# Order of up-projection pieces and down-projection products in the feed-forward part of a hybrid attention layer

## The chip, the cores and the metric

The kernel runs on one core of one Trainium2 chip. The metric is device time in microseconds (us), taken as the median of several runs.

## The reference

One layer of a hybrid encoder, on 256 tokens of width 2048, all in float32. First a mixer with two groups of eight heads (forgetting attention and stick-breaking attention), then the feed-forward part, which the change is about:

```python
def conv_ffn(h, w_up_l, conv_w_l, conv_b_l, w_down_l):
    u = h @ w_up_l                       # (256, 2048) @ (2048, 2 * 5632)
    u = causal depthwise conv of width 3 over tokens, + conv_b_l
    gate, val = jnp.split(u, 2, axis=-1)
    return (jax.nn.silu(gate) * val) @ w_down_l   # (256, 5632) @ (5632, 2048)
...
h = rms_norm(x, ffn_norm[layer])
x = x + conv_ffn(h, w_up[layer], conv_w[layer], conv_b[layer], w_down[layer])
```

## The kernel before

**Numbers in two halves.** Every float32 matrix is used as a high part (a cast to fp32r) and a low part (what the cast left over). A product then takes high x high, high x low and low x high. Weights are split on the chip as they arrive: `split` (L201, L202) casts the raw tile to `w_hi` on ACT, and subtracts it from the raw tile on DVE to get `w_lo`. Activations are kept as pairs, in `hT` (the layer's input, features by tokens) and `g` (the gated features).

**Up-projection.** The 5632 hidden features are taken in six parts of 8 blocks of 128 (the last has 4). For each two blocks there is a gate and a val half, and each of these is one *up-pair*: two *up-pieces*, the first over features 0 to 1023 of the input, the second over 1024 to 2047. A piece (`from_features`) issues 16 high products (L250, 512 columns: both parts of `hT` against `w_hi`) and 16 low products (L257, 256 columns: the high part of `hT` against `w_lo`), all into the tile `pu`. After the second piece, `convolved` and what follows it work on the finished tile: a copy on ACT, an addition (L835) and a multiplication by the token factors on DVE (L837), the three taps on ACT, their sums on DVE (L856), the SiLU or the product with the gate, and the split into high and low parts.

**Down-projection.** Each part's down-projection is done while the next part's up-projection runs. For each half of the output columns, `down_in_seven` forms a 2 x 2 block product with seven products in place of eight. I call the seven A1 to A7 for the first half and B1 to B7 for the second; in the code they are the seven calls of `product`, in order. Each is 12 matmuls (L223) into a PSUM bank. The banks: products 1, 4, 5 and 7 accumulate into `bank_a`, 2 and 6 into `bank_b`, and 3 is `bank_c`. After each product the running sum in its bank is added into, or subtracted from, a block of x by DVE (`added`, L933); the next product on that bank adds to the sum that was read there. Products 2, 4 and 7 use a weight sum, `w_sum`: DVE makes it first (`first_sum`, L986), and two further weights are added into it by accumulating DMAs from the POOL queue (`plus`, L956), which also add into the raw tile of the second weight, used by product 5. Products 2, 4, 5 and 6 take sums of gated features as the other operand (tiles `s`, L898 and L903).

**Order.** All this is a list of steps, each an up-piece or a down-product. The string `ORDER` says how they follow each other in a part (`u` an up-piece, `s` a down-product, a digit the plain down-projection of the last part), `LAST_ORDER` the same for the last part. Letters for which nothing is left are passed over: in the first part there is no `s`. A loop then issues, for step n in the middle, on queues that keep exactly this order:

```python
at(LOAD, 0)      # DMA of the raw weights of step n + 6
follow()         # one move of all that follows finished steps
at(SPLIT, 2)     # split of step n + 2
follow()
at(SUM, 1)       # weight sum of step n + 4
at(0, 3)         # matmuls of step n
```

What follows a step (`convolved`, `added`, and so on) are generators that move on by one `yield` at each `follow()`, the oldest first. There are four raw tiles (`w_raw`), three `w_hi` and three `w_lo`, so the split of step n + 3 goes into the tiles that step n has read. The attention stage before uses `from_features` too, through `feature_major`, in eight pairs of pieces with two `w_hi` and two `w_lo`.

Of the kernel before, what the change touches and what calls it, by code (L numbers as in the profile page):

```python
# [14 lines left out]
P = 128  # L15
D = 2048
S = 256
NT = S // P
KT = D // P
# [18 lines left out]
FFN_PARTS = [(f, min(f + 8, NFT)) for f in range(0, NFT, 8)]  # L38


ORDER = "uuusususususususususususususus"
LAST_ORDER = "uususususususussss0s1ss3s2"


@with_exitstack
def hybrid_layer(
# [19 lines left out]
    nc = tc.nc  # L66
# [65 lines left out]
    hT = big.tile([P, KT, 2, S], F32R, name="hT")  # L132
# [98 lines left out]
    def token_major(lhs, w, k0, nk, c0, cols):  # L231

        acc = psa.tile([P, NT, 512], F32, name="acc", tag="acc")
        for k in range(0, nk, 4):
            parts = weights(rows_of(w, k0 + k, 4, c0, cols), 4, cols)
            in_three(
                [acc[:, t, :cols] for t in range(NT)], parts, 4,
                lambda i, part, t: of_half(lhs(k + i), part, t), k == 0, k + 4 == nk,
            )
            step()  # L240
        return acc

    def from_features(acc, parts, kh, n=8):

        hi, lo = parts
        for i0 in range(0, 8, n):
            for i in range(i0, i0 + n):
                k = 8 * kh + i
                for j in range(2):
                    nc.tensor.matmul(  # L250
                        acc[:, j, :], hi[:, i, j * P : (j + 1) * P],
                        hT[:, k].rearrange("p a b -> p (a b)"), start=k == 0, stop=False,
                    )
            for i in range(i0, i0 + n):
                k = 8 * kh + i
                for j in range(2):
                    nc.tensor.matmul(  # L257
                        acc[:, j, S:], lo[:, i, j * P : (j + 1) * P], hT[:, k, 0, :],
                        start=False, stop=k == KT - 1,
                    )  # L260

    def feature_major(w, c0, pool, tag):

        acc = pool.tile([P, 2, 512], F32, name="pu", tag=tag)
        for kh in range(2):
            from_features(acc, weights(rows_of(w, 8 * kh, 8, c0, 2 * P), 8, 2 * P), kh)
            step()
        return acc
# [9 lines left out]
    with ExitStack() as actx:  # L278
# [9 lines left out]
        def project(c0, cols):  # L288
            return token_major(lambda k: hT[:, k], wi, 0, KT, c0, cols)
# [199 lines left out]
        low = big.tile([P, 2, 16 * P], F32R, name="low", tag="x2")  # L489
# [41 lines left out]
        for j in range(3):  # L531
            acc = project(2 * WF + 344 * j, 344)
            n = 344 if j < 2 else 336
# [206 lines left out]
        for half in range(2):  # L740
            qT = sb_queries(half)
            kT = sb_keys(half)
            acc = project(B0 + 2 * WF + 512 * half, 512)
# [18 lines left out]
        for group in range(2):  # L762
# [3 lines left out]
            for c in range(4):  # L766
                acc = token_major(lambda k: oT[group * NH + k], wo, group * NH, NH, 512 * c, 512)
# [6 lines left out]
                if c == 0:  # L774
                    pg = psb.tile([P, NT], F32, name="pg", tag="t")
                    for t in range(NT):
                        nc.tensor.matmul(
                            pg[:, t : t + 1], ssq[group][:, t * P : (t + 1) * P], ones[:, 0:1],
                            start=t == 0, stop=t == NT - 1,
# [125 lines left out]
    def up_pieces(part, f0, follows):  # L905

        c0 = f0 * P + (DFF if follows is val_follows else 0)
        cell = []

        def piece(kh):  # L910
            mem = {}

            def loads():
                mem["raw"] = load(rows_of(wu, 8 * kh, 8, c0, 2 * P))

            def prepare():
                mem["parts"] = split(mem["raw"], 8, 2 * P)

            def matmuls():
                if kh == 0:  # L920
                    cell.append(psa.tile([P, 2, 512], F32, name="pu", tag="acc"))
                from_features(cell[0], mem["parts"], kh, 8 if c0 else 4)

            new_step(loads, None, prepare, matmuls, (lambda: follows(part, cell[0], f0)) if kh else None)

        piece(0)
        yield
        piece(1)
        yield
# [76 lines left out]
    def down_plain(part, c):  # L1006

        n = (part.f_hi - part.f_lo) // 4

        ends = LAST_ORDER[-1] == str(c // 512)  # L1010
        sizes = [(0, 0, 512), (1, 0, 256), (1, 256, 256)] if ends else [(t, 0, 512) for t in range(NT)]
# [45 lines left out]
    for f_lo, f_hi in FFN_PARTS:  # L1057
# [9 lines left out]
        if f_hi == NFT:  # L1067
            steps_of |= {str(i): [down_plain(part, 512 * i)] for i in range(4)}
        for g in ORDER if f_hi < NFT else LAST_ORDER:
            if steps_of[g]:  # L1070
# [83 lines left out]
```

## Time and profile before

| | before |
|---|---|
| runs | 1107.03, 1107.19, 1107.64 us (median 1107.19) |
| profiled execution, first to last instruction | 1104.9 us |
| PE (matmul) busy | 1099.6 us, 5880 matmuls |
| DVE busy | 870.4 us |
| ACT busy | 706.3 us |

The profiled execution has its span only, from its first to its last instruction; a run's time lies 2.1 to 2.7 us above it (1107.03 to 1107.64 against 1104.9). Times of a row are a start in us after the span's beginning, a length in us, the engine, the line, and what is written from what. PE is the matrix engine, PEld its weight loads, DVE the vector engine, ACT the scalar engine, POOL and SP the engines that issue DMAs. `[2.62 <-PE pu L250]` says that the engine stood idle for 2.62 us before, until PE finished with `pu` at L250. Matmuls are pipelined: a row's length contains the end of the last one, so the pace is read from start to start. In groups, the columns are the count, then busy us and the mean in ns of one, then idle time before and what ended it.

### The profile page before, as it was taken

The page shows a single profiled execution, that of the slowest core. Times are in us where ns is not written, and L with a number is a line of the kernel's source. Part 1 is how long each engine was busy: PE and PEld are TensorE (multiplying, and loading weights), DVE is VectorE, ACT ScalarE, POOL GpSimd, SP SyncE. Part 2 cuts the span into 40 slices and gives each one's busy share as a digit, 9 for nine tenths or more (in the row PEclk, how much of TensorE's full clock was granted, in tenths as well). Part 3 has the DMA queues.
Part 4 walks back from the last instruction along what each step waited for, and adds up shares of the span by engine and source line. Part 5 has one row for each costly group of instructions (what it writes and reads, how often), then busy time and mean ns, then how long its engine had stood idle before and what let it go on. Part 6 is the DMA issues. An engine that isn't in the chain of part 4 may idle for free. (4 is left out here: it accounts for less than half of the span.)

```text
span 1104.9 us, 14836 instructions
## 1 busy us (share of the span) xinstructions
PE 1099.6 (100%) x5880; PEld 953.9 (86%) x5880; DVE 870.4 (79%) x941; ACT 706.3 (64%) x879; POOL 44.0 (4%) x44
## 2 busy tenths in 40 slices
PE   9999999999999999999999999999999999999998
PEld 7998888888888888888888888888888888888887
DVE  6755767667676677679889888889798889889896
ACT  6543555457674567667767776667676677677753
POOL 0000000000000000000000010100000010100010
PEclk9999999999999999999999999999999999999999
DMA  8776555555644396557989597986979689987985
GB/s 285 195 232 229 187 164 180 173 170 169 242 156 158 114 304 200 190 189 195 301 210 323 191 229 264 260 269 178 315 210 306 213 218 281 245 264 196 324 212 168
DMA packets 179407, 246.09 MB, mean 223 GB/s; under 512 B 4432, under 2 KB 118890, under 8 KB 179082
## 3 DMA queue, kind: packets, MB, share of 16 engines
q1 hardware_dynamic: 162458, 209.87, 58.3%
q0 software_dynamic: 16560, 34.75, 16.7%
q8 instruction: 46, 0.75, 0.3%
q10 hardware_dynamic: 320, 0.53, 0.1%
q14 instruction: 23, 0.19, 0.0%
HBM read 243.02 MB, written 2.11 MB: 222 GB/s over the span
## 5 line engine op out<-in xcount | busy, mean ns | idle before, releaser
L202 DVE TENSOR_TENSOR w_lo<-w_raw,w_hi 128x2048 fp32r<-128x2048 f32 (+1 forms) x196 | 439.7, 2246 | 155.0 <-ACT w_hi L201 153.2
L201 ACT CAST w_hi<-w_raw 128x2048 fp32r<-128x2048 f32 (+1 forms) x196 | 367.1, 1875 | 247.4 <-PE pu L250 68.9
L250 PE MATMUL pu<-hT,w_hi 128*128 128x512 f32 x1664 | 396.7, 390 | 0.0
L250 PEld LDWEIGHTS pu<-hT,w_hi 128*128 128x128 f32 x1664 | 309.4, 188 | 62.6
L257 PEld LDWEIGHTS pu<-hT,w_lo 128*128 128x128 f32 x1664 | 213.7, 191 | 8.3
L257 PE MATMUL pu<-hT,w_lo 128*128 128x256 f32 x1664 | 216.4, 283 | 0.0
L223 PE MATMUL acc<-w_hi,hT 128*128 128x512 f32 (+1 forms) x576 | 124.9, 369 | 0.0
L223 PEld LDWEIGHTS acc<-w_hi,hT 128*128 128x128 f32 x576 | 101.2, 188 | 14.2
L201 ACT CAST w_hi<-w_sum 128x2048 fp32r<-128x2048 f32 x30 | 57.2, 1908 | 42.0 <-PE pu L250 35.8
L202 DVE TENSOR_TENSOR w_lo<-w_sum,w_hi 128x2048 fp32r<-128x2048 f32 x30 | 68.7, 2290 | 19.0 <-ACT w_hi L201 19.0
L851 ACT ACTIVATE tap<-up,ccol 128x256 f32<-128x256 f32 x176 | 74.6, 495 | 0.0
L223 PE MATMUL acc<-w_lo,hT 128*128 128x512 f32 (+1 forms) x288 | 64.6, 366 | 0.0
L223 PEld LDWEIGHTS acc<-w_lo,hT 128*128 128x128 f32 x288 | 51.6, 188 | 7.5
L956 POOL DMA_DIRECT2D w_sum<-in_w_down_dram x20 | 25.7, 1284 | 742.8 <-DVE w_lo L202 732.1
L223 PE MATMUL acc<-w_hi,oT 128*128 128x512 f32 x192 | 46.5, 394 | 0.0
L223 PEld LDWEIGHTS acc<-w_hi,oT 128*128 128x128 f32 x192 | 35.4, 188 | 7.2
L223 PE MATMUL bank_a<-w_hi,s 128*128 128x512 f32 x160 | 40.1, 392 | 0.2 <-DVE x L933 0.2
L223 PE MATMUL bank_a<-w_hi,g 128*128 128x512 f32 x160 | 40.0, 392 | 0.0
L223 PE MATMUL bank_b<-w_hi,s 128*128 128x512 f32 x160 | 40.0, 392 | 0.0
L223 PEld LDWEIGHTS bank_a<-w_hi,s 128*128 128x128 f32 x160 | 28.8, 189 | 5.8 <-issue 0.6
L223 PEld LDWEIGHTS bank_a<-w_hi,g 128*128 128x128 f32 x160 | 28.9, 189 | 5.3
L223 PEld LDWEIGHTS bank_b<-w_hi,s 128*128 128x128 f32 x160 | 28.9, 189 | 5.2
(215 smaller groups left out, 1077.5 us busy)
## 6 DMA issues: line engine op xcount, KB each, us to landing
w_raw<-in_w_up_dram SPq DMA_DIRECT2D x88, 1024.0 KB, 7.9
w_raw<-in_w_down_dram SPq DMA_DIRECT2D x44, 1024.0 KB, 6.6
w_raw<-in_w_in_dram SPq DMA_DIRECT2D x36, 1024.0 KB, 5.3
w_sum<-in_w_down_dram POOLq DMA_DIRECT2D x20, 1024.0 KB, 10.3
w_raw<-in_w_out_dram SPq DMA_DIRECT2D x16, 1024.0 KB, 5.1
w_raw<-in_w_down_dram POOLq DMA_DIRECT2D x10, 1024.0 KB, 14.7
w_raw<-in_w_in_dram SPq DMA_DIRECT2D x12, 688.0 KB, 4.3
w_raw<-in_w_in_dram SPq DMA_DIRECT2D x6, 512.0 KB, 7.1
```

The costliest lines, as they stand in the source:

```text
L201: act.copy(hi[:, :n], raw[:, :n])
L202: dve.tensor_tensor(lo[:, :n], raw[:, :n], f32(hi[:, :n]), op=ALU.subtract)
L223: nc.tensor.matmul(o, lhs(i, l, t), r[:, i, :], start=starts and j == 0, stop=stops and j == 3 * n - 1, skip_group_check=more,)
L250: nc.tensor.matmul(acc[:, j, :], hi[:, i, j * P : (j + 1) * P], hT[:, k].rearrange("p a b -> p (a b)"), start=k == 0, stop=False,)
L257: nc.tensor.matmul(acc[:, j, S:], lo[:, i, j * P : (j + 1) * P], hT[:, k, 0, :], start=False, stop=k == KT - 1,)
L851: act.activation(taps[w][:, j, :], u[:, j, w : w + S], AF.Copy, scale=ccol[:, w, f : f + 1])
L956: nc.gpsimd.dma_start(mem[into][:, : nk * 512].rearrange("p (a b) -> p a b", a=nk), src, accum_op=ALU.add)
```

## The change

Two things change. In `from_features` the second piece of a pair (`kh` is 1) issues its low products before its high ones, so that a pair goes high, low, low, high. And the orders are rewritten: the two pieces of a pair follow each other directly, and two down-products stand between pairs, where one stood between pieces.

```diff
-ORDER = "uuusususususususususususususus"
-LAST_ORDER = "uususususususussss0s1ss3s2"
+ORDER = "uuuu" + "ssuu" * 6 + "ss"
+LAST_ORDER = "uussuussuussuussss0s1ss3s2"
...
     def from_features(acc, parts, kh, n=8):
 
         hi, lo = parts
+
+        def high(k, i, j):
+            nc.tensor.matmul(
+                acc[:, j, :], hi[:, i, j * P : (j + 1) * P],
+                hT[:, k].rearrange("p a b -> p (a b)"), start=k == 0, stop=k == KT - 1,
+            )
+
+        def low(k, i, j):
+            nc.tensor.matmul(
+                acc[:, j, S:], lo[:, i, j * P : (j + 1) * P], hT[:, k, 0, :], start=False, stop=False,
+            )
+
         for i0 in range(0, 8, n):
-            for i in range(i0, i0 + n):
-                k = 8 * kh + i
-                for j in range(2):
-                    nc.tensor.matmul(
-                        acc[:, j, :], hi[:, i, j * P : (j + 1) * P],
-                        hT[:, k].rearrange("p a b -> p (a b)"), start=k == 0, stop=False,
-                    )
-            for i in range(i0, i0 + n):
-                k = 8 * kh + i
-                for j in range(2):
-                    nc.tensor.matmul(
-                        acc[:, j, S:], lo[:, i, j * P : (j + 1) * P], hT[:, k, 0, :],
-                        start=False, stop=k == KT - 1,
-                    )
+            for product in (low, high) if kh else (high, low):
+                for i in range(i0, i0 + n):
+                    for j in range(2):
+                        product(8 * kh + i, i, j)
```

## The prediction

> **What bounds the kernel now.** I read the page first (busy times, then the slices), then busy time by stage, then the order of time of each engine in one cycle.
>
> ```profile
> PE 1099.6 (100%) x5880; PEld 953.9 (86%) x5880; DVE 870.4 (79%) x941; ACT 706.3 (64%) x879; POOL 44.0 (4%) x44
> PEclk9999999999999999999999999999999999999999
> ```
> ```profile
> 504.00:621.00 117.00, 117.00 (x625) 101.30 (x624) 103.78 (x94) 84.67 (x95) 7.77 (x6) 1.00 0.90 253
> 631.00:749.00 118.00, 118.00 (x629) 102.17 (x629) 102.59 (x90) 83.94 (x92) 7.74 (x6) 1.00 0.91 254
> ```
> The columns of the second fence are the stage, its length, and the busy time of PE, PEld, DVE, ACT and POOL. In the stages where up-pieces and down-products alternate, PE has no idle time at all and DVE is busy 103.8 of 117.0 us, 89%. So PE sets the time, a microsecond in which PE waits is a microsecond lost, and DVE is the engine that can make it wait.
>
> One cycle on PE, in order of time (start, length, operation):
> ```profile
> 573.55 3.79 PE L250 MATMUL pu<-hT,w_hi 128*128 128x512 f32 x16
> 577.18 2.08 PE L257 MATMUL pu<-hT,w_lo 128*128 128x256 f32 x16
> 579.09 2.00 PE L223 MATMUL bank_c<-w_hi,g 128*128 128x512 f32 x8
> 580.93 1.07 PE L223 MATMUL bank_c<-w_lo,g 128*128 128x512 f32 x4
> 581.84 3.79 PE L250 MATMUL pu<-hT,w_hi 128*128 128x512 f32 x16
> ```
> From start to start: 16 high products 3.63 us, 16 low ones 1.91, so an up-piece is 5.54; a down-product is 2.75. That is 227 ns a high product and 119 ns a low one, through the changes of kind too.
>
> **The change part by part.**
>
> *Low products first: no gain.* The same matmuls and weight loads are issued. A change from high to low and back costs nothing visible (3.63 + 1.91 is 16 x 227 + 16 x 119), so setting two low runs side by side removes nothing. Taken at 0.
>
> *What it moves: the release of w_hi.* A second piece now reads its high half last, so that buffer comes free at the end of the piece, 1.91 us later. How the next split hangs on that release is seen here, on ACT and on DVE:
> ```profile
> 577.38 1.91 ACT L201 CAST w_hi<-w_sum 128x2048 fp32r<-128x2048 f32 x1 [2.62 <-PE pu L250]
> ```
> ```profile
> 579.35 2.29 DVE L202 TENSOR_TENSOR w_lo<-w_sum,w_hi 128x2048 fp32r<-128x2048 f32 x1 [2.27 <-ACT w_hi L201]
> 581.56 0.69 DVE L835 TENSOR_TENSOR t<-pu,t 128x512 f32<-128x512 f32 x1
> 582.28 0.69 DVE L837 TENSOR_TENSOR up<-t,R 128x512 f32<-128x512 f32 x1
> 582.89 0.68 DVE L933 TENSOR_TENSOR x<-x,bank_c 128x512 f32<-128x512 f32 x1
> ```
> The high run ended at 577.18; the cast for the step three places on began 0.20 later; then come, in the order in which they were issued, the subtraction (w_lo), the two operations on the finished up-tile, and the addition of the down-product that ran meanwhile. That addition ends at 583.57, 6.39 us after the release.
>
> *Two down-products in a row: B4 and B5 meet.* The new order pairs the 14 products of a part as A1A2, A3A4, A5A6, A7B1, B2B3, B4B5, B6B7. Of these only B4 and B5 accumulate into the same bank one directly after the other: B4's sum must be added into x (L933) before B5 may write the bank. Up to now an up-piece of 5.54 us lay between. That this wait is real shows near the end, where a step lies between them too and yet:
> ```profile
> 1081.33 0.68 DVE L933 TENSOR_TENSOR x<-x,bank_a 128x512 f32<-128x512 f32 x1
> 1082.16 2.08 PE L223 MATMUL bank_a<-w_hi,s 128*128 128x512 f32 x8 [0.24 <-DVE x L933]
> ```
> PE began 0.15 us after the addition ended. In the new order B4 starts exactly when a second piece ends, that is at the release of its w_hi. What stands on DVE ahead of the addition is then the chain above: cast, subtraction for the next first piece, the two operations on the up-tile just finished. So B5 can start 6.39 + 0.15 = 6.54 us after B4 began, where PE would be free after 2.75: a wait of **3.8 us**. Queued behind B5 on PE stands everything else. It happens once in each of the four parts that use the long order with down-products: 4 x 3.8 = 15.2 us. The last part's order keeps a step between B4 and B5, as before.
>
> Bounds for one such wait. From below, an addition that DVE meets idle:
> ```profile
> 572.65 1.07 PE L223 MATMUL bank_b<-w_lo,s 128*128 128x512 f32 x4
> 573.75 0.69 DVE L933 TENSOR_TENSOR x<-x,bank_b 128x512 f32<-128x512 f32 x1 [0.38 <-PE bank_b L223]
> ```
> Here the next matmul came at 573.55 and the addition ended at 574.44; with 0.15 that is 1.0 us. From above, B4 today:
> ```profile
> 590.13 3.79 PE L250 MATMUL pu<-hT,w_hi 128*128 128x512 f32 x16
> 592.87 0.43 DVE L891 TENSOR_TENSOR gate<-gate 128x256 f32<-128x256 f32 x1
> 593.21 0.68 DVE L933 TENSOR_TENSOR x<-x,bank_a 128x512 f32<-128x512 f32 x1
> ```
> B4 had run out at 590.13, and its addition stood behind earlier DVE work until 593.21, ending at 593.89: 3.9 us with the 0.15. I take 3.8, since the chain is that of the new order itself; a late weight sum (below) adds to it.
>
> *The other six pairs.* Durations of what crowds DVE and ACT, by group (busy us, mean ns):
> ```profile
> L202 DVE TENSOR_TENSOR w_lo<-w_raw,w_hi 128x2048 fp32r<-128x2048 f32 x184 | 420.6, 2289 | 139.2 <-ACT w_hi L201 137.4 <-PE pu L257 1.2
> L986 DVE TENSOR_TENSOR w_sum<-w_raw 128x2048 f32<-128x2048 f32 x10 | 22.9, 2286 | 0.0
> L903 DVE TENSOR_TENSOR s<-gate,s 128x512 fp32r<-128x512 f32 x20 | 12.4, 684 | 0.0
> L898 ACT CAST s<-gate 128x512 fp32r<-128x512 f32 x20 | 10.9, 617 | 0.0
> ```
> Count from the start of a pair of down-products; the second piece after it starts at 2 x 2.75 + 5.54 = 11.04 and now needs its w_lo at once, not 3.63 later. On DVE, with 2.21 from subtraction to next: first piece's w_lo until 4.2, two operations on the up-tile until 5.6, addition until 6.2, second piece's w_lo until 8.4: 2.6 us in hand. In pair A7B1 the weight sum (L986, 2.2) comes between: 10.6, 0.4 in hand. Cost 0; if DVE is later by one more subtraction (2.2), 1.8 x 4 = 7 us.
>
> At the start of the last part A2 comes early: its order opens with one pair of pieces, not two, so A2 meets the sums of gates (L898, L903) of the part before just made. What else stands ahead on DVE there:
> ```profile
> 586.50 1.48 DVE L856 TENSOR_TENSOR val<-val,tap 128x512 f32<-128x512 f32 x2
> 588.02 0.69 DVE L871 TENSOR_TENSOR gate<-gate,val 128x512 f32<-128x512 f32 x1
> 590.89 0.68 DVE L876 TENSOR_TENSOR g<-gate,g 128x512 fp32r<-128x512 f32 x1
> ```
> Counted from B6's start: 8.4 as above, weight sum 10.6, taps and product 12.7, addition 13.3, w_lo 15.5, g's low part and four gate sums of 0.43 17.8, w_lo 20.0; then the first L903 until 20.6. A2 would start at 16.58 + 2.75 = 19.3 and needs it from its second matmul, at 19.6: a wait of 1.1, and 0.3 for the third L903: **1.4 us**, between 0 (DVE 1.4 us earlier) and 4 (one more w_lo ahead).
>
> *DMAs.* Landing times from issue:
> ```profile
> w_sum<-in_w_down_dram POOLq DMA_DIRECT2D x20, 1024.0 KB, 10.3
> w_raw<-in_w_down_dram POOLq DMA_DIRECT2D x10, 1024.0 KB, 14.7
> w_raw<-in_w_up_dram SPq DMA_DIRECT2D x88, 1024.0 KB, 7.9
> ```
> From B2 to B5 there are now five steps (19.3 us) in place of six (24.9). The two POOL transfers behind B2's w_lo are issued 0.75 apart:
> ```profile
> 565.38 1.27 POOL L956 DMA_DIRECT2D w_sum<-in_w_down_dram  x1 [37.28 <-DVE w_lo L202]
> 566.13 1.83 POOL L956 DMA_DIRECT2D w_raw<-in_w_down_dram  x1
> ```
> From A7's start that w_lo ends at 10.6 + taps 1.5 + addition 0.6 + 2.2 = 14.9, so the second is issued at 15.7 and lands at 30.4; B5's cast ends at 32.3, before the cast of the chain above may start, at 2 x 16.58 = 33.2. So 0.9 us in hand; each us beyond goes onto the four waits. SP's loads of up-weights are issued when a raw buffer is freed, at least two steps with one up-piece (over 8 us) ahead of their casts: 0.
>
> *Attention.* The same function runs eight pairs of pieces here.
> ```profile
> 158.56 2.08 PE L257 MATMUL pu<-hT,w_lo 128*128 128x256 f32 x16
> 160.47 0.49 PE L624 MATMUL ps_p<-cs,pr 128*128 128x128 f32 x3
> 167.20 1.17 PE L250 MATMUL pu<-hT,w_hi 128*128 128x512 f32 x4
> ```
> ```profile
> 160.74 2.29 DVE L202 TENSOR_TENSOR w_lo<-w_raw,w_hi 128x2048 fp32r<-128x2048 f32 x1 [1.50 <-ACT w_hi L201]
> ```
> The split of the second piece that starts at 167.20 waits for the high run that ended at 158.56, and is done at 163.03. Released at 160.47, it is done at 164.94, 2.3 us ahead of need. Taken at 0, at most 4.
>
> **Sum.** 15.2 + 1.4 = 16.6 us on the span of 1104.9, so 1121.5; the runs lie 2.3 above the span (median 1107.19): **1123.8 us**. Nothing is gained anywhere to set against it.
>
> **The rivals.**
>
> *More waits.* DVE, at 89%, is late at the second pieces, 7 us as worked out, or the POOL transfer is late: 1131. For it: 0.4 and 0.9 us in hand only. Against: the waits on B5 themselves let DVE catch up. 0.12.
>
> *Short waits.* DVE stands idle when B4 ends: 4 x 1.0, 1111 to 1113. It needs the next piece's split to be done earlier, and w_hi's release forbids it. 0.06.
>
> *The clock falls.* The longest wait of PE in this trace is the one at its start,
> ```profile
> 1.06 2.98 PE L372 MATMUL idle<-zeros 128*128 128x256 bf16 x14 [1.06 <-DVE zeros L362]
> ```
> and the granted clock was full in all slices; now PE would stand for 3.6 to 3.8 us. If it were halved over the next down-product, that would cost 2.75 more each time: 11 us, 1134.8. The Trainium skill (TensorE: Matmul & The Clock Gate, "HAM oscillation — how this bites in real kernels") wants no PE gap above some 3.4 us, since after one idle window the clock is halved; its window runs free, so a gap barely longer than it would seldom cover one, and by the rows there is no fall to show. 0.06.
>
> *Not slower: overtaking.* If the matmuls were put in order by readiness, the next first piece would run ahead of B5 and its 5.54 us cover 3.8: 1107.2, no change. It decides as soon as the wait is under 5.54. Against: at 1082.16 PE stood and waited for its turn. 0.02. Another 0.02 is for a gain that I don't see.
>
> **How the numbers follow.** The forecast has 0.72. Its own range: 4 x 2.5 (the two up-tile operations not ahead of the addition) to 4 x 4.8 (the POOL transfer 1.9 late), plus 0 to 4 for A2, and some of attention's 4: 1117 to 1132, which takes in the case of more waits; outside are the short waits, the clock and no change, some 0.16 with the edges. What a measurement can tell from no change is about 0.2%, 2.2 us: faster 0.02, same 0.02, slower 0.96.
>
> **What would show it.** In the profile after: PE idle about 3.8 us before a run on bank_a at L223 four times, each ended by DVE's x, 15 us in the table of waits; DVE's addition just before it, behind a w_lo; spacings of matmuls unchanged. Wrong if those waits are below 2 us, if PE waits for w_lo or w_hi at L250 or L257 more than a few us in all, or if PEclk drops below 9.

## The result and the profile after

| | before | after |
|---|---|---|
| median of the runs | 1107.19 us (1106.93 to 1107.64) | 1136.52 us (1133.58 to 1138.46) |
| profiled execution, first to last instruction | 1104.9 us | 1134.7 us |

The ratio is 1.0259, 95% interval 1.0248 to 1.0270: slower, as forecast, but by 29.3 us and not by 16.6, and 4.5 us above the upper end of the range.

The page after, busy times and granted clock:
```profile
PE 1109.0 (98%) x5880; PEld 958.4 (84%) x5880; DVE 869.1 (77%) x941; ACT 699.8 (62%) x879; POOL 44.0 (4%) x44
PEclk9999999999999999999998999999999999989999
```
PE is busy 9.4 us longer than before with the same 5880 matmuls, and the clock's row, full before, has slices below 9. From the table of waits (total, times, longest):
```profile
PE bank_a L223 <- DVE x L935: 16.6, 4, 4.6
```
(L935 is L933 of the kernel before.) These are the four waits of B5. Here is the first, on PE, on ACT and on DVE:
```profile
593.49 1.98 PE L223 MATMUL bank_a<-w_hi,s 128*128 128x512 f32 x8
595.30 1.07 PE L223 MATMUL bank_a<-w_lo,s 128*128 128x512 f32 x4
600.92 3.75 PE L223 MATMUL bank_a<-w_hi,s 128*128 128x512 f32 x8 [4.55 <-DVE x L935]
604.47 1.44 PE L223 MATMUL bank_a<-w_lo,s 128*128 128x512 f32 x4
605.74 0.62 PE L248 MATMUL pu<-hT,w_hi 128*128 128x512 f32 x2
```
```profile
592.41 3.71 ACT L201 CAST w_hi<-w_raw 128x2048 fp32r<-128x2048 f32 x2 [4.13 <-DMA w_raw<-in_w_down_dram]
```
```profile
594.35 4.49 DVE L202 TENSOR_TENSOR w_lo<-w_raw,w_hi 128x2048 fp32r<-128x2048 f32 x2 [1.61 <-ACT w_hi L201]
598.76 0.68 DVE L837 TENSOR_TENSOR t<-pu,t 128x512 f32<-128x512 f32 x1
599.48 0.69 DVE L839 TENSOR_TENSOR up<-t,R 128x512 f32<-128x512 f32 x1
600.09 0.68 DVE L935 TENSOR_TENSOR x<-x,bank_a 128x512 f32<-128x512 f32 x1
```
B4 runs from 593.49 to 596.2. Its addition stands on DVE behind two subtractions and the two up-tile operations, and ends at 600.77; PE begins 0.15 later. Then B5 itself, 12 matmuls that take 2.72 us in B4, takes 4.82 (600.92 to 605.74). Busy time by stage says why; the columns are the stage, its length, busy PE, PEld, DVE, ACT and POOL, then the granted clock (the last two, the DMA share and GB/s, are not used here):
```profile
598.38:605.20 6.82, 4.28 (x10) 3.44 (x11) 5.85 (x7) 3.58 (x8) 0.00 (x0) 0.50 1.09 285
734.91:738.33 3.42, 3.42 (x10) 2.67 (x9) 2.71 (x3) 2.11 (x5) 0.00 (x0) 0.50 1.09 264
868.03:871.45 3.42, 3.42 (x10) 2.65 (x9) 2.26 (x3) 1.39 (x4) 0.00 (x0) 0.50 1.08 290
997.74:1004.57 6.83, 4.22 (x10) 3.38 (x11) 5.93 (x7) 3.60 (x8) 0.00 (x0) 0.50 1.09 284
```
At each of the four waits the granted clock fell to half, for 3.4 or 6.8 us.

**Where the 29.8 us of the span went**, from start to start of matmuls:

| | us |
|---|---|
| four waits of B5 beyond the 227 ns pace: 4.71, 3.85, 3.98, 4.74 | 17.3 |
| matmuls at half clock behind them (427 ns each in place of 227) | 7.4 |
| A2 in the last part, for the sums of gates | 1.4 |
| a second piece in the last part, for w_lo | 0.7 |
| plain down-projection of the last part, for g (1.0) and the last B5 for w_hi (1.3, 0.4 before) | 1.9 |
| a later start of the feed-forward steps (421.81 against 421.01 at the same matmul) | 0.8 |
| smaller waits less smaller gains, and what I could not assign | about 0.3 |

Rows of PE for A2, for the second piece, and for the plain down-projection:
```profile
1037.15 1.19 PE L223 MATMUL bank_b<-w_hi,s 128*128 128x512 f32 x4 [1.20 <-DVE s L905]
1062.83 0.86 PE L254 MATMUL pu<-hT,w_lo 128*128 128x256 f32 x5 [0.51 <-DVE w_lo L202]
1099.19 1.66 PE L1031 MATMUL acc<-w_hi,g 128*128 128x512 f32 x6 [0.84 <-DVE g L878]
```
(The idle time in brackets is counted from the modelled end of a matmul, some 0.16 us after the next could have started.)

### The profile page after: what moved, and what is told of

Same layout as the page of the kernel before. It is cut to its first block, busy times and chain, and to the rows that moved or that the text cites. A ratio compares the mean times of both kernels' runs of the same rounds, so it can differ in the third digit from the quotient of the medians.

```text
span 1134.7 us, 14827 instructions
## 1 busy us (share of the span) xinstructions
PE 1109.0 (98%) x5880; PEld 958.4 (84%) x5880; DVE 869.1 (77%) x941; ACT 699.8 (62%) x879; POOL 44.0 (4%) x44
## 3 DMA queue, kind: packets, MB, share of 16 engines
HBM read 243.02 MB, written 2.11 MB: 216 GB/s over the span
## 5 line engine op out<-in xcount | busy, mean ns | idle before, releaser
L254 PEld LDWEIGHTS pu<-hT,w_lo 128*128 128x128 f32 x1664 | 207.4, 191 | 5.2 <-DVE w_lo L202 1.0
L254 PE MATMUL pu<-hT,w_lo 128*128 128x256 f32 x1664 | 210.6, 283 | 0.6 <-DVE w_lo L202 0.5
L201 ACT CAST w_hi<-w_sum 128x2048 fp32r<-128x2048 f32 x30 | 57.1, 1903 | 23.8 <-PE pu L248 17.3
L223 PE MATMUL bank_a<-w_hi,s 128*128 128x512 f32 x160 | 45.2, 430 | 17.8 <-DVE x L935 16.6
L223 PEld LDWEIGHTS bank_a<-w_hi,s 128*128 128x128 f32 x160 | 32.7, 207 | 26.7 <-issue 18.2
L846 ACT ACTIVATE gate<-up,ccol 128x256 f32<-128x256 f32 x44 | 24.1, 595 | 32.8 <-DVE up L839 29.5
L846 ACT ACTIVATE val<-up,ccol 128x256 f32<-128x256 f32 x44 | 24.1, 595 | 22.4 <-DVE up L839 22.3
```

The source lines that it names most:

```text
L201: act.copy(hi[:, :n], raw[:, :n])
L223: nc.tensor.matmul(o, lhs(i, l, t), r[:, i, :], start=starts and j == 0, stop=stops and j == 3 * n - 1, skip_group_check=more,)
L254: nc.tensor.matmul(acc[:, j, S:], lo[:, i, j * P : (j + 1) * P], hT[:, k, 0, :], start=False, stop=False,)
L846: act.activation(a[:, j, :], u[:, j, 2:], AF.Identity, scale=ccol[:, 2, f : f + 1], bias=ccol[:, 3, f : f + 1],)
```

## The experiments

The theory after the result: nearly all of it is B5's wait, which is set by what DVE has queued ahead of B4's addition, and the clock, which falls because PE stands. Rivals: the low-first order or the pairing costs by itself (late w_hi, w_lo needed at once, bursts of splits); the waits come from the shared bank whatever stands on DVE; the clock falls for a reason other than standing.

### Low products first, in the old order

```diff
-ORDER = "uuuu" + "ssuu" * 6 + "ss"
-LAST_ORDER = "uussuussuussuussss0s1ss3s2"
+ORDER = "uuusususususususususususususus"
+LAST_ORDER = "uususususususussss0s1ss3s2"
```
(against the kernel after)

> The old order of steps, with the low products first in each second piece. If the loss of 29.8 us comes from B5 waiting for B4's addition (17.3 us of waits in the trace after, plus some 8 us of matmuls at half clock behind them), this kernel has none of it: 1107.2, within 1.5. If it comes from the late release of w_hi and from w_lo being needed at once, PE waits at L254 for DVE's w_lo or at L248 for ACT's w_hi and the time is 1110 or more.

Measured 1111.95 us against 1107.04, ratio 1.0043 (1.0030 to 1.0055). So low-first costs 4.9 us on its own; the first expectation fell. Most of it is in the last part. There a second piece asks for its w_lo 3.6 us sooner than before, and stands 1.4 us from start to start:
```profile
1021.93 0.39 PE L254 MATMUL pu<-hT,w_lo 128*128 128x256 f32 x1 [1.20 <-DVE w_lo L202]
```
The other waits are those at the plain down-projection and the last B5 (1.0 and 1.3, as in the kernel after), and 0.8 before one B5 in a long part: 4.4 in four waits, of which the last B5 had 0.4 before.

### The new order, with high products first

```diff
-ORDER = "uuusususususususususususususus"
-LAST_ORDER = "uususususususussss0s1ss3s2"
+ORDER = "uuuu" + "ssuu" * 6 + "ss"
+LAST_ORDER = "uussuussuussuussss0s1ss3s2"
```
(against the kernel before)

> The new order of steps, with high products first everywhere. w_hi of the second piece is then free 1.91 us before B4 starts, so the cast, the subtraction, the two up-tile operations and the addition run that much earlier. Theory of the DVE queue: each of the four waits on B5 falls from 3.9 to 4.7 us to about 1.9 to 2.8; the clock falls after some of them or none; 1115 to 1124. If the waits do not hang on the release of w_hi, they stay near 4.3 and the time near 1136.

Measured 1119.24, ratio 1.0107 (1.0091 to 1.0122), as the theory had it. The four waits are 2.48, 2.11, 2.36 and 2.63 us from start to start beyond the pace, 9.6 in all in place of 17.3. The first of them:
```profile
598.33 2.96 PE L223 MATMUL bank_a<-w_hi,s 128*128 128x512 f32 x8 [2.32 <-DVE x L933]
```
Freeing w_hi 1.91 us earlier took 1.6 to 2.2 us off each wait, 1.9 in the mean. So the wait is the chain from w_hi's release to the addition, and not a fixed price of the shared bank. The clock fell after two of the four.

Alone, the two changes cost 4.9 and 12.2 us; together they cost 29.3. The 12.2 beyond their sum lie in B5's waits (17.3 in place of 9.6) and in the matmuls at half clock (7.4 in place of 3.1).

### B4 and B5 apart, A7B1B2 together

```diff
-ORDER = "uuuu" + "ssuu" * 6 + "ss"
+ORDER = "uuuu" + "ssuu" * 3 + "sssuussuussuus"
```

> As after, but the pairs of a part are A1A2, A3A4, A5A6, then A7B1B2 together, B3B4, B5B6, and B7 alone, so that an up-pair lies between B4 and B5. Theory of the B4 to B5 wait: no wait on bank_a by DVE's x in the four long parts, clock 1.000, what is left are the waits of the last part (about 4.4 us in the trace after) and up to 2 at the group of three: 1108 to 1114. If pairing as such is what costs (bursts of splits on DVE), PE waits at L248 and L254 and the time stays above 1120.

Measured 1128.30, ratio 1.0187 (1.0171 to 1.0203): far above the expectation. The waits on bank_a by DVE's x are gone, but two others have come, in the table of waits:
```profile
PE pu L254 <- DVE w_lo L202: 9.3, 4, 4.4
PE bank_b L223 <- DVE s L905: 4.5, 1, 4.5
```
The first come once in each long part, at the second piece behind B3B4, one pair later than the group of three. DVE is not late there: it is idle and waits for ACT, and ACT waits for the weights of that piece. Here are ACT, DVE and PE in the second part:
```profile
719.15 1.90 ACT L201 CAST w_hi<-w_raw 128x2048 fp32r<-128x2048 f32 x1 [5.87 <-DMA w_raw<-in_w_up_dram]
721.08 2.29 DVE L202 TENSOR_TENSOR w_lo<-w_raw,w_hi 128x2048 fp32r<-128x2048 f32 x1 [4.03 <-ACT w_hi L201]
723.42 3.78 PE L254 MATMUL pu<-hT,w_lo 128*128 128x256 f32 x16 [4.40 <-DVE w_lo L202]
```
SP had issued that load at 701.45, 17.7 us before the cast began; in the kernel before, such loads landed after 7.9 us (median). Why the transfers were so slow in this order no run shows. The wait on bank_b is A2 of the last part: there DVE works without a pause, and ends the first L905 only at 1028.9, just before PE goes on. The clock fell three times behind these waits. So this run shows that B5's wait goes when B4 and B5 are apart, but it puts another wait, for a load, in its place, and settles nothing about pairing.

### The wait filled with matmuls

```diff
+                if (bank, to) == ("bank_a", (1, 1)) and c0 and part.f_lo < 32:
+                    spare = psb.tile([P, 512], F32, name="spare", tag="t")
+                    for _ in range(12):
+                        nc.tensor.matmul(
+                            spare, hT[:, 0, 0, :P], hT[:, 0].rearrange("p a b -> p (a b)"), start=True, stop=True
+                        )
                 in_three([mem[bank]], mem["parts", bank, to], nk, lhs(), new, True, more=not new)
```

> As after, with 12 matmuls of 512 columns into a spare bank (their result is not used) put between B4 and B5 in the four long parts. They fill 2.7 us of the 3.9 to 4.7 us in which PE stood. The waits on DVE's x, counted from B4's end, stay as they are. If the clock falls because PE stands still, it now stays at 1.000 and the 8 us behind the waits are gone: 1127 to 1130. If the clock falls for another reason (the order of matmuls, their current), it falls all the same: 1136 or more.

Measured 1128.37, ratio 1.0192 (1.0178 to 1.0206). The time is as expected of the standing theory, the clock not quite: in the profiled execution it fell once, behind the longest wait that was left (in two of the four runs its mean was 0.998, in the others 1.000).
```profile
600.31 2.62 PE L223 MATMUL bank_a<-w_hi,s 128*128 128x512 f32 x8 [1.82 <-DVE x L935]
```
```profile
598.23:601.64 3.41, 1.59 (x8) 1.14 (x7) 3.38 (x5) 2.04 (x5) 0.00 (x0) 1.00 1.11 244
601.64:605.05 3.41, 3.41 (x10) 2.64 (x9) 2.40 (x4) 2.00 (x3) 0.00 (x0) 0.50 1.08 337
```
PE was idle for 1.82 of 3.41 us, and the next 3.41 ran at half. A second kernel had `range(20)`:

> As after, with 20 matmuls of 512 columns into a spare bank between B4 and B5 (4.5 us, about the length of the wait; their result is not used). The waits for B4's addition are as before, only covered. If the clock falls because PE stands, it cannot fall here: clock 1.000, no products at 427 ns, 1128 to 1131. If it falls for another reason, it falls again: 1136 or more.

Measured 1129.90, ratio 1.0206 (1.0190 to 1.0221), clock 1.000 in the profiled execution.
```profile
595.96 4.70 PE L981 MATMUL spare<-hT 128*128 128x512 f32 x20
600.99 2.06 PE L223 MATMUL bank_a<-w_hi,s 128*128 128x512 f32 x8 [0.33 <-DVE x L935]
```
B5 starts as late as in the kernel after (600.99 against 600.92) and yet runs at full pace. Work whose result nobody uses made the kernel 6.6 us faster than the kernel after: the clock fell because PE stood. (The two profiled executions lie 5.8 apart: the 7.4 at half clock, less 1.6 by which B5 starts later in all, since 20 matmuls are longer than the two short waits.)

### B4's addition ahead on DVE

```diff
+            if n in early:
+                at(LOAD, 0)
+                follow()
+                at(0, 3)
+                follows = at(0, 4)
+                next(follows)
+                following.append(follows)
+                at(SPLIT, 2)
+                follow()
+                at(SUM, 1)
+                continue
```
(`early` holds the steps that are B4 in a long part; `next(follows)` issues the addition, ahead of the split and the up-tile.)

> As after, but in the four long parts B4's addition is issued ahead of the split and the up-tile operations that stood before it on DVE. Theory of the DVE queue: each wait of B5 falls to about 1.0 us (the addition met by an idle DVE), no window of the clock is lost, and the time is 1136.5 less 13 (waits) less 8 (half clock): 1113 to 1118. If the waits come from B4 and B5 sharing a bank and not from what stands ahead on DVE, they stay above 3 us.

Measured 1115.75, ratio 1.0079 (1.0065 to 1.0092), clock 1.000. DVE and PE at the same place:
```profile
596.25 0.68 DVE L936 TENSOR_TENSOR x<-x,bank_a 128x512 f32<-128x512 f32 x1
596.84 2.29 DVE L202 TENSOR_TENSOR w_lo<-w_raw,w_hi 128x2048 fp32r<-128x2048 f32 x1
```
```profile
597.07 2.06 PE L223 MATMUL bank_a<-w_hi,s 128*128 128x512 f32 x8 [1.00 <-DVE x L936]
```
The subtraction now stands behind the addition. The four waits are 1.16, 1.03, 1.03 and 1.07 us, 4.3 in all. The same products on the same bank: what they cost is what DVE does first. 20.8 us of the 29.3 are gone by this alone.

### B5B6B7 together

```diff
-ORDER = "uuuu" + "ssuu" * 6 + "ss"
+ORDER = "uuuu" + "ssuu" * 5 + "suusss"
```

> As after, but the end of a part's order is B4 alone, an up-pair, then B5B6B7. B4 and B5 are apart; between B5 and B7, which share the bank, lies only B6 (2.75 us). By the chain of 6.54 us from B5's start, B7 may wait 6.54 - 5.5 = 1.0: 4 us in all, no fall of the clock, and the 4 to 5 us that low products first cost in the last part: 1113 to 1117. If it is pairing as such that costs, 1120 or more.

Measured 1116.95, ratio 1.0094 (1.0080 to 1.0107). B7 waits four times, 1.07 each from start to start, where 1.0 was worked out:
```profile
PE bank_a L223 <- DVE x L935: 3.6, 4, 0.9
```
The rest is in the last part and at the end.

> The same order with high products first everywhere. w_hi is free 1.91 us earlier, the chain from B5's start is 4.6 us, so B7 does not wait (it would start at 5.5); left is about 1 us at the very end: 1107 to 1109. If the pairs of steps still cost by bursts of splits on DVE, 1111 or more.

Measured 1111.53, ratio 1.0040 (1.0027 to 1.0052), 2.5 us above the expectation and where the rival of bursts on DVE had put it. But in the four long parts PE does not wait; three waits (1.3, 1.4, 1.6) all lie in the last part. With the last part's order put back as it was:

> High products first, pairs of down-products between up-pairs in the four long parts with B5B6B7 at their end, and the last part's order as before the change. If pairing costs only where a product meets another on its bank, or where the last part runs out of time for its splits, nothing is left: 1106.5 to 1107.7, the same as before. If pairs cost by bursts of splits on DVE, 1109 or more.

Measured 1110.44, ratio 1.0037 (1.0023 to 1.0050). That missed too, and again on the rival's side. All waits of half a us or more are again in the last part:
```profile
PE bank_a L223 <- DVE x L933: 1.6, 1, 1.6
PE bank_a L223 <- ACT w_hi L201: 1.1, 1, 1.1
PE acc L1029 <- DVE g L876: 0.4, 1, 0.4
```
So pairs by themselves cost nothing in the long parts, where up-pieces cover the splits. The last part is written as in the kernel before, so its waits come from what the order ahead of it leaves behind; on which engine, I did not test. Why the end of the last part keeps 1.3 us here I did not follow further. None of these kernels beats the kernel before, and in the trace there was little to win: in the 643 us of feed-forward steps from 420 to 1063 PE was busy all the time.

## Why the prediction was right and wrong

**B4 and B5 on one bank: right, with some luck in the size.** The place, the number of waits and what ends them were right, and 3.85 and 3.98 us in the second and third of the four parts stand against 3.8 worked out. But DVE had two subtractions ahead of the addition, and the working counted one. On ACT, DVE and PE in the second part:
```profile
727.95 1.92 ACT L201 CAST w_hi<-w_raw 128x2048 fp32r<-128x2048 f32 x1 [0.27 <-PE pu L248]
```
```profile
727.71 4.50 DVE L202 TENSOR_TENSOR w_lo<-w_raw,w_hi 128x2048 fp32r<-128x2048 f32 x2 [0.75 <-ACT w_hi L201]
```
```profile
734.28 3.21 PE L223 MATMUL bank_a<-w_hi,s 128*128 128x512 f32 x8 [3.69 <-DVE x L935]
```
B5 starts 6.57 us after the release at 727.71, where 6.54 was worked out. B5's own subtraction, left out of the working, ran beside the cast of the chain and ended just as that cast did (729.9), so that leaving it out cost nothing here; that is luck. In the first and the fourth part the second POOL transfer landed late, B5's cast waited for it (the row at 592.41), and its subtraction began 0.86 and 0.90 us after the release. The second subtraction stands behind it, and the waits grew by as much, to 4.71 and 4.74, nearly the bound of 4.8 that was given for a late transfer. So the 0.9 us in hand were not there in all parts, and 15.2 became 17.3.

**The clock: the step that failed.** It was a rival with 0.06, priced at 11 us, 1134.8. It happened after every one of the four waits in the profiled execution (the mean clock of the five runs was 0.991 to 0.995), and cost 7.4. I had argued that the gap must cover a whole window of 3.4 us, and so would seldom do. The runs show less is needed. The falls lie on a fixed grid: 598.38, 734.91, 868.03 and 997.74 are 40, 39 and 38 steps of 3.413 us apart. In the window that ends at a fall, PE had stood for 2.17, 2.78, 2.32 and 2.13 us in the kernel after, and for as little as 2.0 in the kernel with 12 fillers (counted from start to start); windows with up to 1.8 us of standing were not followed by a fall, and one with 2.11 (high-first) was not either. So about 60% of a window can be enough, and a wait of 3.8 us puts 1.9 or more into one window wherever the grid lies, close to that border at worst. The Trainium skill (TensorE: Matmul & The Clock Gate, "What's actually happening") gives a free-running window of 3413 ns; the grid agrees. Its "≥1 idle window" must not be read as a window without any matmul: here 2.0 us of standing were enough, and the measurement decides against the limit of 3.4 us that the prediction went by.

Without the clock the time would have been near 1129 (the kernel with 20 fillers: 1129.9), inside the range.

**Low products first at 0: wrong by 4.9 us.** I took the gain as nothing and the later release of w_hi as part of B5's chain alone. That the release of w_hi sets the waits was right (high-first took 1.9 us off them in the mean). Missed was the last part, which I costed only at A2. There low-first alone brought 3.2 us of waits more than before (1.4, 1.0, and 1.3 where 0.4 stood). The gain is not quite nothing either: eight high products right behind a low run took 1.84 us (579.09 to 580.93), behind a high run 1.81 (593.49 to 595.30). The new order has half as many such changes, some 1 us in all.

**A2 in the last part: right,** 1.4 worked out and 1.36 measured. **Second pieces in the long parts: right.** The 0.4 us in hand behind A7B1 held; the largest wait of a second piece was 0.3, behind an A3A4. **Attention: right at 0,** as far as these runs can tell: the feed-forward steps run 0.8 us later, but 0.5 of it stood at 4 us already, ahead of any up-piece.

**Overtaking:** PE kept its order; it stood in front of B5 from 596.2 on, with the cast of the next piece's weights done at 596.12 (the second of the row at 592.41).

## What to carry to other kernels

When two products that share an accumulator are moved next to each other, the wait between them is not the read-out itself (1.0 us here) but everything that the reading engine has queued ahead of it (3.9 to 4.7); follow that queue from the moment its first buffer comes free. Two cures did about the same: issuing the read-out first on that engine took away 20.8 us of 29.3, and more distance on PE (B4 alone, B5B6B7 together) 19.6. And where PE is always busy, price a wait of about 2 us or more twice, once for the wait and once for the clock behind it.

## What was not expected of the hardware

The granted clock halved after a window of 3.41 us in which PE stood for about 2 us or more (with one exception, at 2.11), with matmuls at 427 ns in place of 227; it came back after one window in which PE was busy throughout. Filling the wait with 20 unused matmuls kept it at full, and made the kernel 6.6 us faster.
